# Gated halves added on VectorE and stored plainly, evictions of a down product given out over the next one, the last quarters' running sum on VectorE

## The chip, the cores and the metric

The kernel runs on one core of one Trainium2 chip. The metric is the device time of one execution in microseconds (us); smaller is better. The kernel before takes 1638.05 us (median of three runs, 1633.67 to 1639.48). The execution that the profiler recorded took 1630.3 us, of which 1628.5 us are the span from the first instruction to the last.

A core has five engines with a queue of instructions each: TensorE (PE in the profile; PEld are its weight loads), VectorE (DVE), ScalarE (ACT), GpSimd (POOL) and SyncE (SP). An engine works through its own queue in order; between queues only semaphores order the work. A DMA is issued by one of the queues and runs beside them.

## The reference

One layer of a diffusion backbone: two attention branches over 1024 tokens of 1024 channels, merged and normalized, and then a gated convolutional feed-forward part. Only the feed-forward part and the last normalization are touched:

```python
def _conv_ffn(h, w_up, conv_w, conv_b, w_down):
    u = h @ w_up                                   # 1024 x 1024 @ 1024 x 5632
    u = lax.conv_general_dilated(u, conv_w, ...) + conv_b   # 3 taps along the tokens
    gate, val = jnp.split(u, 2, axis=-1)           # 2816 channels each
    return (jax.nn.silu(gate) * val) @ w_down      # 1024 x 2816 @ 2816 x 1024
...
h = x * (1.0 + scale2) + shift2
y = _conv_ffn(h, w_up[l], conv_w[l], conv_b[l], w_down[l])
x = _layer_norm(DEEPNORM_ALPHA * x + gate2 * y, ln2_g[l], ln2_b[l])
```

All of it is float32. The kernel makes a float32 product of three reduced ones: each operand is split into a high part (a cast on ScalarE) and a low part (a subtraction), and TensorE runs high x high, low x high and high x low (L90, L91, L92 in `mm3`).

## The kernel before

**Up projection.** The 2816 channels of gate and of value are 22 pairs of tiles of 128 channels, j = 0 to 21; a pair is called a tile below. Tiles 0 to 2 are computed directly (`up_conv`). From tile 3 on `up_tile` computes gate, value and both halves of the tokens with seven products of quarter size in place of eight (Strassen's scheme in Winograd's form): A11, S2, S1, S3, A12, S4, A22, each four times three matmuls of 512 columns, 84 for a tile. They land in four banks of PSUM, a, b, c, d. S2 and S1 use operands T2 and T1 that `build` prepares once; T2 and T4 of channel block k stand in the tiles T24h and T24l (high and low), whose cast is L1113. A12 adds to bank a, so it waits until ScalarE has copied A11 out (L1368, `pv<-a`).

Behind its products, a tile needs on VectorE the sums of the banks (L1356), for gate (`tg`) and value (`tv`) the three taps (L1231 on ScalarE, L1232 and L1234 on VectorE), Silu (L1386), and the product of both (L1243 or L1249, in `gated`). On GpSimd it needs one sum (`uv<-uv,pv`, L1356), the low parts of two weights (L87) and four sums of weights for the next tile but one (`s<-ru`, L1075). The raw weights `ru` come by two DMAs of SP (L1325) when their buffers are free.

**Gated values.** For the down projection, which runs in seven products in the same way, DRAM holds the operands: `td[j]` has four slots of 128 x 512 for a tile j below 11. With lo and hi for the two halves of the tokens, slot 0 is lo, slots 1 and 2 are lo+hi, slot 3 is hi. The kernel before writes lo into slots 0, 1 and 2, hi into 3, by SP (L1244, L1245), and then has GpSimd issue a DMA that adds hi to slots 1 and 2 in DRAM (L1247; L1305 for tiles 0 to 2, after all three). That DMA waits until the stores have landed. Tiles 11 to 21 go negated into `g2d`, and GpSimd's DMA (L1251) adds their hi to slots 2 and 3 of tile j-11; it waits only for VectorE's product.

**Down projection.** `product(p)` runs for p = 1, 6, 2, 7, 4, 5, each 11 steps k of four output blocks f, 132 matmuls of 512 columns, into four banks; the next product takes the other four. The seventh product, 3, comes last in two quarters of 256 tokens (`last_mm`, tiles `yl`). For each step two tiles are loaded (`rd`, L1208 and L1209), cast on ScalarE (`hd`, L82) and subtracted on VectorE (`ld`, L87), three steps ahead (`dnext`). The eleven pairs of product 3 are loaded at places that `D3AT` lists as (product, step), the others after product 5. After a product its four banks are evicted: f by f added to the outputs `zz` (L1417 and L1423), with running sums of the values (`zs`, L995, on GpSimd) and of the squares (`zq`, L994 and L996) for the normalization.

**Normalization.** `ln_steps` yields steps (statistics by TensorE, L1028 and L1029; a broadcast, L1044; then for each f L1051 on VectorE, L1053 on GpSimd or VectorE, L1410 on ScalarE and a store) that `tick` interleaves with the matmuls: each has a delay in model nanoseconds (`LN2_D`, 640 of them for three matmuls). The first half of the tokens (b0) runs under product 5. The last 256 tokens are transposed by TensorE (`tok`, tiles `zt`) into banks of product 5.

Only TensorE's queue stands as written. The other queues are ordered by a scheduler that takes instructions as it expects them to be ready. Slots of SBUF (`ht` takes one, `hput` gives it back) go round: who takes a slot waits for its last readers, DMAs among them.

Of the kernel before, what the change touches and what calls it, by code (L numbers as in the profile page):

```python
# [10 lines left out]
ALU = mybir.AluOpType  # L11
# [16 lines left out]
HALF = 512  # L28
# [7 lines left out]
SPAN = 0.8, 0.85  # L36
LN1_F = 3500.0, 2000.0, 2000.0
LN1_D = (2500.0, 2000.0, 2000.0, 2500.0), (2500.0, 2000.0, 1000.0, 700.0), (2500.0, 2000.0, 1000.0, 700.0)
LN2_D = 16000.0, 5000.0, 2500.0, 1500.0, 700.0
LN2_E = 3500.0, 3000.0, 1500.0, 800.0, 500.0  # L40
NCL = 3
BLD = 2400.0
# [3 lines left out]
GORD = 3, 4, 4, 1, 4  # L46
PWB = 5
DAH = 3
D3AT = (7, 1), (7, 4), (7, 7), (4, 1), (4, 4), (4, 7), (5, 0)
NXS = 5  # L50
RAWB = 3
OTP = (0, 0), (1, 0)
# [7 lines left out]
LN2_P = 1, 2, 2  # L60
# [9 lines left out]
def layer_kernel(  # L70
# [6 lines left out]
    nc = tc.nc  # L77
# [44 lines left out]
    NH = NF // 2  # L122
    td = [dpool.tile([P, 4, HALF], F32, tag=f"td{j}", name=f"td{j}") for j in range(NH)]
# [104 lines left out]
    acc = [acc_tile(f"q1acc{t}") for t in range(NT)]  # L228
# [715 lines left out]
    for f in range(2, KT):  # L944
# [4 lines left out]
        for j in range(4):  # L949
            k = (f % 2) * 4 + j  # L950
# [35 lines left out]
    def ln_add(zf, zs, zq, s, first, nm, qe, se):  # L986
        w = s.stop - s.start
        ln_flush()
        if first:
            nc.scalar.activation(zq[:, s], zf, AF.Square)  # L990
            nc.gpsimd.tensor_scalar(out=zs[:, s], in0=zf, scalar1=1.0, scalar2=0.0, op0=ALU.mult, op1=ALU.add)
            return
        q = tm(f"sq{nm}", w=w)
        nc.scalar.activation(q, zf, AF.Square)  # L994
        se.tensor_tensor(out=zs[:, s], in0=zs[:, s], in1=zf, op=ALU.add)  # L995
        sqs.append(lambda: qe.tensor_tensor(out=zq[:, s], in0=zq[:, s], in1=q, op=ALU.add))  # L996
# [204 lines left out]
    def dload(p, k, mk):  # L1201
        w, g = dsrc(p, k)
        n = nraw[0] % (3 + len(xs))
        nraw[0] += 1
        pool, tag, bufs = (post, "raw", 3) if n < 3 else (*xs[n - 3], 1)
        r = pool.tile([P, 2, HALF], F32, tag=tag, name=f"rd{p}_{k}", bufs=bufs)
        o = r[:, 0]
        nc.sync.dma_start(o.rearrange("p (a b) -> p a b", b=P) if len(w.shape) == 3 else o, w)  # L1208
        nc.sync.dma_start(r[:, 1], g)  # L1209
        if p == 2:  # L1210
            nc.gpsimd.dma_start(td[k][:, 2], r[:, 1], accum_op=ALU.add)
        h, l = (mk(f"{a}d{p}_{k}", (P, 2, HALF), R32) for a in "hl")
        split(r, h, l, nc.scalar, nc.vector)
        return h, l
# [22 lines left out]
    def twice(a, n=2):  # L1237
        return a.unsqueeze(1).to_broadcast([P, n, HALF])

    def gated(j, tg, tv):  # L1240
        lo, hi = tg[:, 0:HALF], tg[:, HALF:T]
        if j < NH:
            nc.vector.tensor_tensor(out=tg, in0=tg, in1=tv, op=ALU.mult)  # L1243
            nc.sync.dma_start(td[j][:, 0:3], twice(lo, 3))  # L1244
            nc.sync.dma_start(td[j][:, 3], hi)  # L1245
            if j >= NCL:
                nc.gpsimd.dma_start(td[j][:, 1:3], twice(hi), accum_op=ALU.add)  # L1247
# [53 lines left out]
    for j in range(NCL):  # L1301
        up_conv(j)
    drain()
    for j in range(NCL):
        nc.gpsimd.dma_start(td[j][:, 1:3], twice(td[j][:, 3]), accum_op=ALU.add)  # L1305
    hput(*[f"B{k}_1" for k in range(4)])


# [130 lines left out]

    sides = [banks[0:4], banks[4:8]]  # L1440
    nside = [0]
    d3 = []
    h0, h1 = hsl(0), hsl(1)

    def product(p):
        tags = sides[nside[0] % 2]
        nside[0] += 1
        acc = [ps4.tile([P, HALF], F32, tag=f"r{n}", name=f"p{p}_{f}") for f, n in enumerate(tags)]
        for k in range(NH):
            dnext()  # L1450
# [22 lines left out]
    zs2, zq2 = tm("zs2"), tm("zq2")  # L1473

    def sums(f, s, first):
        ln_add(zv(f, s), zs2, zq2, s, first, f"b{f}_{s.start}", nc.vector, nc.gpsimd)

    for p in (1, 6, 2, 7, 4, 5):
        if p == 6:
            for hf in (0, 1):  # L1480
                for k in range(4):
                    for a in (0, 1):
                        nc.sync.dma_start(zt_[k, hf][:, a], zd[k + 4 * a][:, hsl(hf)])
            for a in (0, 1):
                nc.sync.dma_start(lnr[a], ln2_row[a].partition_broadcast(P))
        if p == 5:
            banks[:] = sides[nside[0] % 2 ^ 1]
        acc = product(p)
        for f in range(4):
            o = acc[f]  # L1490
            if p == 1:
                nc.scalar.copy(u2[f], o)
            elif p == 6:
                accum(f, h0, u2[f], False)
                nc.vector.tensor_tensor(out=u2[f], in0=u2[f], in1=o, op=ALU.subtract)
            elif p == 2:
                accum(f, h0, o, True)
                sums(f, h0, f == 0)
                accum_affine(f, h1, u2[f], True)
            elif p == 7:  # L1500
                nc.vector.tensor_tensor(out=u3[f], in0=u2[f], in1=o, op=ALU.add)
# [8 lines left out]
        if p == 7:  # L1510
            hput("u20", "u21", "u30", "u31")
        if p == 4:
            pend += ln_steps(zs2, zq2, h0, "b0", emit2, *LN2_D, LN2_P[0])
    for f in range(4):
        accum(f, h1, acc[f], True)
    banks[:] = sides[nside[0] % 2] + sides[nside[0] % 2 ^ 1]
    d3 += [dload(3, k, ring) for k in range(len(D3AT), NH)]

    s = LN2_S[-1]
    w = s.stop - s.start  # L1520
# [187 lines left out]
```

## Time and profile before

| | |
|---|---|
| median of three runs | 1638.05 us |
| profiled execution | 1630.3 us, span 1628.5 us |
| PE busy in the span | 1542.9 us (95%) |
| DVE, ACT, POOL busy | 1209.8, 811.2, 721.8 us |
| up projection, tiles 3 to 21 | about 998 to 1395 us from the span's start |
| down products 1, 6, 2, 7, 4, 5 | about 1395 to 1574 us |
| last quarters and output | about 1574 to 1628 us |

In a row of the timeline the first number is the start in us from the span's start, the second the duration; a bracket at the end gives the idle time of the engine ahead of the row and what ended it. Several instructions of one kind in a row are merged (x2). In a row of windows the stretch comes first, then its length, then busy time and number of instructions of PE, PEld, DVE, ACT and POOL, then the granted clock of TensorE, the busy share of the DMA engines and GB/s. Names are those of the program, without numbers.

### The profile page before, as it was taken

To read this page: it belongs to the slowest core of one execution; us is meant where nothing else is said; L and a number is where in the kernel's file an instruction comes from. 1 tells how busy PE (TensorE), PEld (TensorE's weight loads), DVE (VectorE), ACT (ScalarE), POOL (GpSimd) and SP (SyncE) were. 2 spreads that over 40 slices of the span, in tenths; PEclk is the share of its full clock that TensorE was granted. 3 is DMA by queue.
4 is the path that set the end of the run, shared out by engine and by line. 5 is a ranking of instruction groups with operands and counts; after the bars stand their busy time and mean duration, and the time that the engine had idled before them with its cause. 6 is when DMAs were issued, how large, how long until landed. Compare 5 with 4: busy or idle time off the path is not lost.

```text
span 1628.5 us, 22043 instructions
## 1 busy us (share of the span) xinstructions
PE 1542.9 (95%) x7680; PEld 1275.9 (78%) x7680; DVE 1209.8 (74%) x1748; ACT 811.2 (50%) x1443; POOL 721.8 (44%) x749
## 2 busy tenths in 40 slices
PE   6999999999999999999999989999999999999895
PEld 5878788888877887777788877877778888888785
DVE  7796646548887677888756695799988887657775
ACT  5422222368887667787223563434345444445532
POOL 0563303426665556665225344544447664021133
PEclk9999999999999999999999999999999999999998
DMA  9685662322255655531540324344444447997522
GB/s 379 217 315 182 218 202 82 113 78 59 60 147 126 149 123 137 111 68 44 176 155 27 104 78 128 108 108 123 130 104 107 120 114 189 361 266 232 183 96 72
DMA packets 115184, 235.76 MB, mean 145 GB/s; under 512 B 12960, under 2 KB 27808, under 8 KB 114976
## 3 DMA queue, kind: packets, MB, share of 16 engines
q1 hardware_dynamic: 96640, 198.93, 36.6%
q0 software_dynamic: 13392, 25.96, 10.4%
q10 hardware_dynamic: 5040, 9.46, 1.6%
q8 instruction: 60, 0.98, 0.2%
q14 instruction: 52, 0.43, 0.1%
HBM read 178.93 MB, written 71.63 MB: 154 GB/s over the span
## 4 chain that ended last, share of the span: by engine, by line
PE 62%; DVE 17%; DMA 7%; ACT 6%; issue 5%; POOL 3%; SPq 1%; ACTq 0%; DVEq 0%; POOLq 0%
PE ptr L531 4%; DVE tg L1232 4%; PE p L91 3%; PE p L92 2%; PE p L90 2%; PE g L90 2%; PE g L91 2%; PE g L92 2%; PE b L92 2%; PE b L91 2%; PE b L90 2%; DMA wml<-in_wmodT_dram 2%; PE s L414 2%; PE av L552 2%; PE av L553 2%
## 5 line engine op out<-in xcount | busy, mean ns | idle before, releaser
L541 DVE TENSOR_TENSOR ptl<-ptr,pth 128x512 fp32r<-128x512 f32 x188 | 124.6, 684 | 27.8 <-ACT pth L540 25.1
L87 DVE TENSOR_TENSOR ld<-rd,hd 128x1024 fp32r<-128x1024 f32 x77 | 95.0, 1249 | 57.9 <-ACT hd L82 51.5
L531 PE MATMUL ptr<-ident,p 128*128 128x128 f32 x816 | 126.8, 278 | 9.6 <-DVE ptl L541 7.1
L540 ACT CAST pth<-ptr 128x512 fp32r<-128x512 f32 x188 | 106.6, 588 | 56.4 <-PE ptr L531 32.7
L426 ACT ACTIVATE p<-p,nm 128x1024 f32<-128x1024 f32 (+2 forms) x128 | 125.3, 981 | 11.4 <-DVE p L459 10.6
L82 ACT CAST hd<-rd 128x1024 fp32r<-128x1024 f32 x77 | 80.3, 1051 | 98.9 <-PE p L92 73.8
L531 PEld LDWEIGHTS ptr<-ident,p 128*128 128x128 f32 x816 | 93.7, 140 | 40.0 <-DVE ptl L541 14.3
L91 PE MATMUL p<-ld,hd 128*128 128x512 f32 x264 | 103.5, 392 | 5.4 <-DVE ld L87 5.4
L1232 DVE SCALAR_TENSOR_TENSOR tg<-ug,cvt,tg 128x1023 f32<-128x1023 f32 x19 | 88.6, 4665 | 25.4 <-ACT tg L1231 25.4
L552 PE MATMUL av<-pth,VT 128*128 128x512 f32 x236 | 104.6, 443 | 1.0 <-ACT avs L558 0.5
L90 PE MATMUL p<-hd 128*128 128x512 f32 x264 | 103.7, 393 | 0.0
L92 PE MATMUL p<-hd,ld 128*128 128x512 f32 x264 | 103.2, 391 | 0.0
L90 PE MATMUL g<-hh,whg 128*128 128x512 f32 x256 | 99.9, 390 | 0.0
L92 PE MATMUL g<-hh,wlg 128*128 128x512 f32 x256 | 99.7, 389 | 0.0
L91 PE MATMUL g<-hl,whg 128*128 128x512 f32 x256 | 99.6, 389 | 0.0
L553 PE MATMUL av<-ptl,VT 128*128 128x512 f32 x236 | 97.7, 414 | 2.0 <-POOL ptl L87 1.8
L87 POOL TENSOR_TENSOR wlg<-wg,whg 128x512 fp32r<-128x512 f32 x32 | 44.7, 1403 | 110.3 <-ACT whg L82 110.3
L459 DVE TENSOR_SCALAR_CACHE_REDUCE p<-s,cvt,nmc 128x1024 f32<-128x1024 f32 x64 | 84.4, 1339 | 12.3 <-PE s L415 11.8
L414 PE MATMUL s<-KL,q 128*128 128x512 f32 (+2 forms) x192 | 76.0, 396 | 2.9 <-ACT p_x L426 2.0
L188 DVE CUSTOM_DVE_ANT_0 wml<-wml,sc,bmc 128x1024 f32<-128x1024 f32 x32 | 45.2, 1422 | 38.4 <-DMA wml<-in_wmodT_dram 38.2
L90 PE MATMUL a<-B,wA 128*128 128x512 f32 x152 | 61.8, 406 | 11.5 <-ACT pv L1368 11.5
L415 PE MATMUL s<-KL,q 128*128 128x512 f32 (+2 forms) x192 | 71.6, 373 | 0.0
(395 smaller groups left out, 4926.1 us busy)
## 6 DMA issues: line engine op xcount, KB each, us to landing
wml<-in_wmodT_dram SPq DMA_DIRECT2D x48, 512.0 KB
ru<-in_w_up_dram SPq DMA_DIRECT2D x38, 512.0 KB
rd<-td SPq DMA_DIRECT2D x55, 256.0 KB
rd<-sd SPq DMA_DIRECT2D x44, 256.0 KB
td<-tg POOLq DMA_DIRECT2D x19, 512.0 KB, 6.5
rd<-in_w_dn_dram SPq DMA_DIRECT2D x33, 256.0 KB
wm<-in_wmodT_dram SPq DMA_DIRECT2D x16, 512.0 KB
wg<-in_w_g_dram SPq DMA_DIRECT2D x32, 256.0 KB
```

The costliest lines, as they stand in the source:

```text
L87: lo_eng.tensor_tensor(out=lo, in0=src, in1=hi.bitcast(F32), op=ALU.subtract)
L90: nc.tensor.matmul(ps, a[0], b[0], start=start, stop=False, skip_group_check=resumed)
L91: nc.tensor.matmul(ps, a[0], b[1], start=False, stop=False, skip_group_check=resumed)
L92: nc.tensor.matmul(ps, a[1], b[0], start=False, stop=stop, skip_group_check=resumed)
L414: nc.tensor.matmul(o, self.q[0][:, hs], ks, start=True, stop=False)
L426: nc.scalar.activation(p, s, AF.Exp, bias=nm[:, h:h + 1], scale=scale, accum_out=sm[:, h:h + 1])
L531: nc.tensor.transpose(tr[:, h * P:(h + 1) * P], self.pslice(h, n), ident)
L540: nc.scalar.copy(hi, tr)
L541: nc.vector.tensor_tensor(out=lo, in0=tr, in1=hi.bitcast(F32), op=ALU.subtract)
L552: nc.tensor.matmul(self.av, v, hi, start=first, stop=False)
L553: nc.tensor.matmul(self.av, v, lo, start=False, stop=self.left == 0)
L1232: nc.vector.scalar_tensor_tensor(out=t[:, 1:T], in0=u[:, 0:T - 1], scalar=cvw[:, c, 0:1], in1=t[:, 1:T], op0=ALU.mult, op1=ALU.add)
```

## The change

There are three parts and two changed lists.

- `gated` (tiles 0 to 10): VectorE adds lo and hi into the first half of `tv`; SP stores lo into slot 0, hi into slot 3 and the sum into slots 1 and 2. The DMAs that GpSimd issued to add in DRAM (L1247 and L1305) are gone, eleven in all.
- Down products: the four evictions of a product are kept as a list and written into the next product, one at each odd step k (at each step of product 5), behind that step's loads. The normalization of b0 starts when product 4's evictions are given out. The evictions of product 5 are still written out behind it.
- The running sum `zs` of the last two quarters goes from GpSimd to VectorE.
- `LN2_D` and `D3AT` have new values that belong to the second part.

```diff
-LN2_D = 16000.0, 5000.0, 2500.0, 1500.0, 700.0
+LN2_D = 5000.0, 4000.0, 2500.0, 1500.0, 700.0
-D3AT = (7, 1), (7, 4), (7, 7), (4, 1), (4, 4), (4, 7), (5, 0)
+D3AT = (7, 5), (7, 9), (4, 1), (4, 4), (4, 7), (4, 10), (5, 2)
...
         if j < NH:
             nc.vector.tensor_tensor(out=tg, in0=tg, in1=tv, op=ALU.mult)
-            nc.sync.dma_start(td[j][:, 0:3], twice(lo, 3))
+            nc.vector.tensor_tensor(out=tv[:, 0:HALF], in0=lo, in1=hi, op=ALU.add)
+            nc.sync.dma_start(td[j][:, 0], lo)
             nc.sync.dma_start(td[j][:, 3], hi)
-            if j >= NCL:
-                nc.gpsimd.dma_start(td[j][:, 1:3], twice(hi), accum_op=ALU.add)
+            nc.sync.dma_start(td[j][:, 1:3], twice(tv[:, 0:HALF]))
...
-    for j in range(NCL):
-        nc.gpsimd.dma_start(td[j][:, 1:3], twice(td[j][:, 3]), accum_op=ALU.add)
...
             if (p, k) in D3AT:
                 d3.append(dload(3, len(d3), ht))
+            if evict and (k % 2 or p == 5):
+                evict.pop(0)()
+            if not evict and after:
+                after.pop()()
...
-        ln_add(zv(f, s), zs2, zq2, s, first, f"b{f}_{s.start}", nc.vector, nc.gpsimd)
+        ln_add(zv(f, s), zs2, zq2, s, first, f"b{f}_{s.start}", nc.vector,
+               nc.vector if s.start else nc.gpsimd)
...
-        for f in range(4):
-            o = acc[f]
+
+        def ev(f, o, p=p):
             if p == 1:
                 nc.scalar.copy(u2[f], o)
...
+        evict += [lambda f=f, o=acc[f]: ev(f, o) for f in range(4)]
         if p == 4:
-            pend += ln_steps(zs2, zq2, h0, "b0", emit2, *LN2_D, LN2_P[0])
+            after.append(lambda: pend.extend(ln_steps(zs2, zq2, h0, "b0", emit2, *LN2_D, LN2_P[0])))
+    banks[:] = sides[nside[0] % 2] + sides[nside[0] % 2 ^ 1]
+    d3 += [dload(3, k, ring) for k in range(len(D3AT), NH)]
+    for e in evict:
+        e()
     for f in range(4):
         accum(f, h1, acc[f], True)
```

Three places in the queues matter below. The first is ScalarE's queue at the start of tile 3, with what each row waits for in the brackets (`DVE`, `PE`, `Pool`, `Activation` are engines, `DMAHW` are DMAs of SP). `c0_2` and `c1_2` are gate and value of tile 2, `pv3` the copy of tile 3's bank a, T24h_3 the cast of T2 and T4 for channel block 3. Before:

```order
L1231 ACTIVATE c1_2_10449<-u1_2_10386,cvt_70 128x1024 [waits PE_49]
L82 CAST wA11_4_10589<-ru0_4_10565 128x512 [waits DMAHW0_49]
L1113 CAST T24h_3_10467<-t24_3_10460 128x1024 [waits DVE_49,Activation_49]
L1368 COPY pv3_10512<-a3_10508 128x512 [waits PE_49]
L82 CAST wS2_4_10622<-s12_4_10569 128x512 [waits Pool_49]
```

With the change:

```order
L1231 ACTIVATE c1_2_10453<-u1_2_10390,cvt_70 128x1024 [waits PE_49]
L82 CAST wA11_4_10592<-ru0_4_10568 128x512 [waits DMAHW0_49]
L1366 COPY pv3_10515<-a3_10511 128x512 [waits PE_49]
L82 CAST wS2_4_10625<-s12_4_10572 128x512 [waits Pool_49]
L1113 CAST T24h_3_10473<-t24_3_10466 128x1024 [waits DMAHW3_49,DVE_49,Activation_49]
```

The cast of T24h_3 moved behind two rows and gained a wait for a DMA: its slot is that of value tile `c1_2`, which the new store reads.

The second is VectorE's queue where product 7 ends and product 4 begins: `u30`, `u31`, `zz` are evictions of product 7, `ld4_k` the low part for step k of product 4, `ld3_k` for product 3. Before, from the fifth eviction of product 7 on (the four ahead of it follow `ld4_1` and `ld3_5`):

```order
L1417 SCALAR_TENSOR_TENSOR zz1_0_13217<-u30_13225,nmod_13211,zz1_0_13217 128x512
L1423 SCALAR_TENSOR_TENSOR zz1_1_13218<-zz1_1_13218,lnx_69,ya5_14186 128x512
L1501 TENSOR_TENSOR u31_13226<-u21_13224,p7_2_13947 128x512
L1501 TENSOR_TENSOR u31_13226<-u21_13224,p7_3_13948 128x512
L1417 SCALAR_TENSOR_TENSOR zz2_0_13219<-u31_13226,nmod_13211,zz2_0_13219 128x512
L1417 SCALAR_TENSOR_TENSOR zz3_0_13221<-u31_13226,nmod_13211,zz3_0_13221 128x512
L1423 SCALAR_TENSOR_TENSOR zz2_1_13220<-zz2_1_13220,lnx_69,ya6_14191 128x512
L1423 SCALAR_TENSOR_TENSOR zz3_1_13222<-zz3_1_13222,lnx_69,ya7_14196 128x512
L87 TENSOR_TENSOR ld4_2_14207<-rd4_2_14203,hd4_2_14206 128x1024
```

With the change:

```order
L87 TENSOR_TENSOR ld4_1_14168<-rd4_1_14164,hd4_1_14167 128x1024
L1504 TENSOR_TENSOR u30_13236<-u20_13234,p7_0_13927 128x512
L87 TENSOR_TENSOR ld4_2_14191<-rd4_2_14187,hd4_2_14190 128x1024
L1415 SCALAR_TENSOR_TENSOR zz0_0_13226<-u30_13236,nmod_13222,zz0_0_13226 128x512
L1421 SCALAR_TENSOR_TENSOR zz0_1_13227<-zz0_1_13227,lnx_69,ya4_14222 128x512
L87 TENSOR_TENSOR ld4_3_14210<-rd4_3_14206,hd4_3_14209 128x1024
L1504 TENSOR_TENSOR u30_13236<-u20_13234,p7_1_13928 128x512
L1504 TENSOR_TENSOR u31_13237<-u21_13235,p7_2_13929 128x512
```

Before, all twelve evictions stood ahead of `ld4_2`; now one does.

The third is VectorE's queue where product 5 ends (`rbb0` is b0's broadcast, `p5_f` a bank of product 5, `modc` and `nmod` the gains for its two evictions). Before, from the fifth of the eight L1051 on, and then with the change, from the eighth on:

```order
L1051 TENSOR_TENSOR zz0_0_13215<-zz0_0_13215,rbb0_14663 128x512
L1417 SCALAR_TENSOR_TENSOR zz0_1_13216<-p5_0_14453,modc_60,zz0_1_13216 128x512
L1417 SCALAR_TENSOR_TENSOR zz1_1_13218<-p5_1_14454,modc_60,zz1_1_13218 128x512
L1417 SCALAR_TENSOR_TENSOR zz2_1_13220<-p5_2_14455,modc_60,zz2_1_13220 128x512
L1417 SCALAR_TENSOR_TENSOR zz3_1_13222<-p5_3_14456,modc_60,zz3_1_13222 128x512
```

```order
L1051 TENSOR_TENSOR zz3_0_13232<-zz3_0_13232,rbb0_14646 128x512
L1415 SCALAR_TENSOR_TENSOR zz0_1_13227<-p5_0_14444,modc_60,zz0_1_13227 128x512
L87 TENSOR_TENSOR ld3_7_14745<-rd3_7_14741,hd3_7_14744 128x1024
L87 TENSOR_TENSOR ld3_8_14752<-rd3_8_14748,hd3_8_14751 128x1024
L87 TENSOR_TENSOR ld3_9_14759<-rd3_9_14755,hd3_9_14758 128x1024
L87 TENSOR_TENSOR ld3_10_14766<-rd3_10_14762,hd3_10_14765 128x1024
L1415 SCALAR_TENSOR_TENSOR zz1_1_13229<-p5_1_14445,modc_60,zz1_1_13229 128x512
```

All eight L1051 now stand ahead of product 5's first eviction (five before), and the last four `ld3` behind that first one. In ScalarE's queue the casts `hd3_7` to `hd3_10` moved behind the eight output rows of b0 in the same way.

More of the change, by code (lines that the diff above doesn't have):

```diff
@@ L1441, in layer_kernel @@
     nside = [0]
-    d3 = []
+    d3, evict, after = [], [], []
     h0, h1 = hsl(0), hsl(1)
@@ L1503, in layer_kernel @@
                 accum_affine(f + 4, h1, u3[f], False)
+                if f == 3:
+                    hput("u20", "u21", "u30", "u31")
             elif p == 4:
@@ L1509, in layer_kernel @@
                 sums(f + 4, LN2_S[1], f == 0)
-        if p == 7:
-            hput("u20", "u21", "u30", "u31")
+        evict += [lambda f=f, o=acc[f]: ev(f, o) for f in range(4)]
         if p == 4:
-            pend += ln_steps(zs2, zq2, h0, "b0", emit2, *LN2_D, LN2_P[0])
+            after.append(lambda: pend.extend(ln_steps(zs2, zq2, h0, "b0", emit2, *LN2_D, LN2_P[0])))
[3 more added lines that the diff above has]
+        e()
     for f in range(4):
         accum(f, h1, acc[f], True)
-    banks[:] = sides[nside[0] % 2] + sides[nside[0] % 2 ^ 1]
-    d3 += [dload(3, k, ring) for k in range(len(D3AT), NH)]
     s = LN2_S[-1]
```

## Prediction

> **What bounds the kernel now.** First the page's parts on busy time and on the chain that ended last:
>
> ```profile
> PE 1542.9 (95%) x7680; PEld 1275.9 (78%) x7680; DVE 1209.8 (74%) x1748; ACT 811.2 (50%) x1443; POOL 721.8 (44%) x749
> PE 62%; DVE 17%; DMA 7%; ACT 6%; issue 5%; POOL 3%; SPq 1%; ACTq 0%; DVEq 0%; POOLq 0%
> PE ptr L531 4%; DVE tg L1232 4%; PE p L91 3%; PE p L92 2%; PE p L90 2%; PE g L90 2%; PE g L91 2%; PE g L92 2%; PE b L92 2%; PE b L91 2%; PE b L90 2%; DMA wml<-in_wmodT_dram 2%; PE s L414 2%; PE av L552 2%; PE av L553 2%
> ```
>
> TensorE is busy 95% of the span, so all there is to win is in its 85.6 us of gaps and in matmuls that run at a lower clock. One VectorE line, L1232, holds 4% of the chain. So the next view is the windows from one `tg` L1232 to the next, which is one tile of the up projection each (tiles 3, 5, 6, 10, 11; the last row holds the eight tiles 13 to 20):
>
> ```profile
> 1021.41:1040.45 19.04, 19.04 (x85) 15.77 (x84) 14.19 (x14) 9.26 (x13) 10.65 (x8) 1.00 0.47 125
> 1059.49:1080.64 21.15, 19.65 (x86) 15.72 (x85) 19.75 (x14) 8.89 (x13) 9.18 (x8) 1.00 0.44 114
> 1080.64:1103.81 23.17, 20.78 (x85) 16.71 (x84) 20.61 (x14) 8.89 (x13) 11.34 (x11) 0.93 0.47 131
> 1168.04:1191.49 23.45, 20.86 (x85) 16.72 (x84) 20.81 (x15) 8.88 (x13) 11.59 (x11) 0.93 0.50 130
> 1191.49:1212.02 20.53, 19.64 (x86) 15.69 (x85) 19.14 (x14) 8.88 (x13) 11.44 (x10) 1.00 0.44 91
> 1230.96:1383.50 152.54, 152.54 (x674) 126.36 (x673) 126.92 (x110) 72.88 (x101) 98.10 (x60) 1.00 0.50 130
> ```
>
> Tiles 13 to 20 take 152.54/8 = 19.07 us each with TensorE never idle (152.54/674 = 0.226 us a matmul). Tiles 5 to 11 take 20.5 to 23.5 with the same matmuls. Why, the timeline shows at tile 6:
>
> ```profile
> 1077.40 0.68 DVE L1356 TENSOR_TENSOR uv<-d,uv 128x512 f32<-128x512 f32 x1
> 1078.75 0.33 SPq L1325 DMA_DIRECT2D ru<-in_w_up_dram  x1
> 1079.91 1.19 POOL L1247 DMA_DIRECT2D td<-tg  x1 [11.97 <-DMA td<-tg]
> 1080.69 1.74 POOL L1356 TENSOR_TENSOR uv<-uv,pv 128x512 f32<-128x512 f32 x1
> 1088.17 1.68 POOL L1075 TENSOR_TENSOR s<-ru,s 128x512 f32<-128x512 f32 x1
> 1080.64 10.30 DVE L1232 SCALAR_TENSOR_TENSOR tg<-ug,cvt,tg 128x1023 f32<-128x1023 f32 x1 [1.36 <-ACT tg L1231]
> 1090.87 0.68 DVE L1356 TENSOR_TENSOR uv<-d,pv 128x512 f32<-128x512 f32 x1
> 1094.41 0.68 PE L90 MATMUL a<-B,wA 128*128 128x512 f32 x1 [2.39 <-ACT pv L1368]
> 1094.89 0.63 PE L91 MATMUL a<-B,wA 128*128 128x512 f32 x1
> ```
>
> GpSimd stands 11.97 us at its DMA until the stores have landed. Then its seven other rows run without a gap, one each 1.25 us ((1088.17-1080.69)/6), and L1232, which starts 0.05 us before the first of them, lasts 10.30 us: it ends 1.1 us after GpSimd's last. Everything behind it on VectorE is late, so ScalarE's second tap and `pv` behind that, and TensorE waits 2.39 us for `pv`; then its matmuls start every 0.43-0.48 us for a while in place of 0.226. Tile 17 has the same rows without that backlog:
>
> ```profile
> 1303.83 1.59 POOL L1356 TENSOR_TENSOR uv<-uv,pv 128x512 f32<-128x512 f32 x1 [1.05 <-DVE uv L1356]
> 1305.39 1.29 POOL L87 TENSOR_TENSOR wS<-s,wS 128x512 fp32r<-128x512 f32 x1
> 1307.13 1.28 DVE L1232 SCALAR_TENSOR_TENSOR tg<-ug,cvt,tg 128x1023 f32<-128x1023 f32 x1 [1.36 <-ACT tg L1231]
> 1309.43 1.92 POOL L1075 TENSOR_TENSOR s<-ru 128x512 f32<-128x512 f32 x1 [2.75 <-DMA ru<-in_w_up_dram]
> 1304.33 13.54 SPq L1325 DMA_DIRECT2D ru<-in_w_up_dram  x2
> ```
>
> GpSimd's sum follows VectorE's at once, the low part follows, and then GpSimd waits for `ru`, issued at 1304.33 and landed 5.1 us later. In that hole L1232 takes 1.28 us.
>
> **The change, part by part. Gated values, tiles 3 to 12.** The DMA leaves GpSimd's queue. In tile 6 its sum could then start at 1078.1, when VectorE's is done (1077.40 + 0.68), and the low part would end at 1080.6; the hole of tile 17 follows, and L1232 (1080.64) falls into it. VectorE gets one sum of 128x512 more per tile, 0.68 us by the L1356 row. It works 14.2 us of 19.04 in tile 3's window, so TensorE covers it; without cover it would cost 9 x 0.68 = 6.1 us. SP gets a third store, a little under 0.5 us of issue; the next `ru` waits for a split that comes later anyway. From tile 3's L1232 to tile 12's it is 1212.02-1021.41 = 190.6 us now; nine periods of 19.07 are 171.6. Gain **19.0**. If every second tile still stalled, half, 9.5.
>
> The Trainium skill, page "SBUF — State Buffer", section "SBUF: two separate sides", says that VectorE instructions with two SBUF inputs and GpSimd share one port pair by an exclusive lock, held "for the whole instruction". By that rule L1232 would wait for one GpSimd row at most, 1.7 us, and 6.5 of its 10.30 us would have another cause; then this term would be about nil in place of 19.0, which is a rival below. The trace speaks against it: the wait spans all seven rows.
>
> **The price of the stored sum, tile 3.** ScalarE's cast of T24h_3 now waits until the store that reads `c1_2` has landed. Rows at that place (`td<-c` are tile 2's stores):
>
> ```profile
> 1002.69 1.22 DVE L1243 TENSOR_TENSOR c<-c,c 128x1024 f32<-128x1024 f32 x1
> 1004.37 0.48 SPq L1245 DMA_DIRECT2D td<-c  x1
> 1008.81 1.14 POOL L1305 DMA_DIRECT2D td<-td  x1 [9.01 <-DMA td<-c]
> 1004.00 1.04 ACT L1113 CAST T24h<-t 128x1024 fp32r<-128x1024 f32 x1 [3.95 <-DVE c L1243]
> 1005.10 0.50 PE L90 MATMUL b<-T24h,wS 128*128 128x512 f32 x1 [2.33 <-ACT T24h L1113]
> ```
>
> TensorE waits here already. The third store issues behind the second (1004.85) and takes 0.48: 1005.3. Stores landed 1008.81-1004.85 = 4.0 us after their last issue: 1009.3. The cast then starts 5.3 us later than 1004.00, and nothing covers it: **+5.3**. In later tiles the landing took less (tile 6: 1079.91 is 3.3 us after the last issue), `ru` took 5.1: +4.6 to +6.4. Behind the cast on ScalarE stand casts for tile 4, which are not needed for 20 us. T24h_2 and T24l_1 get such waits too, but earlier, and TensorE reaches them 10 us and more later: nil.
>
> **Evictions given out.** The waits of the down stage (1395 to 1628 us), and the windows around product 7's end and the last quarters:
>
> ```profile
> PE p L91 <- DVE ld L87: 5.4, 2, 4.5
> PE stb L1028 <- POOL zs L995: 2.2, 1, 2.2
> 1505.96 1.28 DVE L1501 TENSOR_TENSOR u<-u,p 128x512 f32<-128x512 f32 x2
> 1513.66 5.75 DVE L87 TENSOR_TENSOR ld<-rd,hd 128x1024 fp32r<-128x1024 f32 x5
> 1510.00:1530.00 20.00, 15.49 (x62) 12.37 (x61) 14.31 (x15) 7.92 (x10) 0.00 (x0) 0.91 0.61 203
> 1580.00:1600.00 20.00, 17.40 (x142) 16.91 (x142) 13.54 (x26) 6.18 (x10) 9.28 (x10) 0.99 0.14 52
> ```
>
> Product 7's twelve evictions hold VectorE from 1505.96 to 1513.66, the low parts of product 4 come late, and TensorE waits 4.5 us; with the slow matmuls behind, 62 are done in 20 us where 20/0.226 = 88 fit: 26 x 0.226 = 5.9 us lost. With one eviction (three rows, 2 us) per two steps (5.4 us) between the low parts, which are made two steps ahead, this goes: **-5.9**; if loads of product 3, one more of which falls into product 4, make VectorE wait there, half of it stays, -3. The other wait, 5.4-4.5, follows product 2 and goes too: **-0.9**.
>
> **The end.** VectorE's queue there is worse. Rows now:
>
> ```profile
> 1567.84 0.86 PE bcrb L1044 x2
> 1570.26 7.95 POOL L1053 TENSOR_TENSOR zz<-zz,mbb 128x512 f32<-128x512 f32 x5 [8.00 <-ACT mbb L1046]
> 1571.88 0.82 ACT L1410 ACTIVATE of<-zz,ln2c 128x512 f32<-128x512 f32 x1 [1.70 <-POOL zz L1053]
> 1575.73 2.72 DVE L1417 SCALAR_TENSOR_TENSOR zz<-p,modc,zz 128x512 f32<-128x512 f32 x4
> 1583.41 2.34 DVE L87 TENSOR_TENSOR ld<-rd,hd 128x1024 fp32r<-128x1024 f32 x2
> ```
>
> I count from E, the end of product 5. Now seven passes of three matmuls (4.8 us) and the broadcast (1.7) lie between 1567.84 and E = 1574.3; with the change fourteen passes do, so b0's broadcast starts at E-11.2, GpSimd's L1053 2.4 later (1570.26-1567.84) at E-8.8, and eight of them at 7.95/5 = 1.59 end at E+3.9. ScalarE's last output row ends at E+4.7, then `hd3_7` (1.05) and on VectorE four `ld3` at 1.17 (2.34/2): E+10.4. TensorE needs them after 84 matmuls at 17.40/142 = 0.1225, E+10.3 to E+11.4: just in time. But three more evictions of product 5, with six small sums of about 0.4 between, and two of the other sign, 0.68 each, stand behind them: E+16.2. TensorE wants those two banks for its transposes at E+11.8: a wait of 4.4 us that is not there now. The wait of 2.2 for `zs` goes in exchange, since TensorE comes later than VectorE's sums (eight of 0.4 us, covered by that wait; uncovered 3.2). I take **+2.0**, between -2.4 (old wait gone, none new) and +6 (L1053 slower, and slow matmuls behind).
>
> **Sum.** -19.0 + 5.3 - 5.9 - 0.9 + 2.0 = -18.5. Made against the profiled execution's 1630.3 us it gives 1611.8. The median of the runs shown lies 7.75 above that execution, and the changed kernel will be timed like those, so I forecast 1638.05 - 18.5 = **1619.5 us**.
>
> **Rivals.** *Half the gain*: GpSimd still meets L1232 in every second tile, because `ru` comes at another moment. For it: tiles 7, 9 and 11 stalled less than 6, 8 and 10, so the state of one tile depends on the one ahead. Against it: eight tiles in a row run clean without the store wait. 1638.05 - 9.0 = 1629.
>
> *The lock-out stays and the sum adds to it* (slower side): L1232's length isn't GpSimd's backlog. Place: tiles 4 to 11, VectorE between `ug` and `uv<-d,pv`. It decides if `ru` lands less than 1.9 us (1080.6-1078.75, SP's issue behind the split in tile 6) after its issue, or if one row's hold was never the cause. Then the 19.0 are lost and the extra sum lies on the stalled path, +6.1: 5.3 - 5.9 - 0.9 + 2.0 + 6.1 = +6.6, 1644.7, and 1648.7 with the end at its upper bound. Against it: 5.1 us in the `ru` row. The "SBUF — State Buffer" page's rule would lead here.
>
> *The prices don't come*: the cast at tile 3 and the end are hidden. -25.8, which is 1612, less some of the -2.4: 1611. For it: my count at the end rests on rows of other moments.
>
> *It doesn't do what it says* for evictions (the scheduler puts them ahead of the loads again): the order in VectorE's queue excludes this for product 4.
>
> **Chances.** Forecast 0.72, half the gain 0.10, prices don't come 0.13, lock-out stays 0.05. About 0.5% (8 us) is what a measurement of this kernel can tell from no change. Faster by more: forecast, third rival and most of the first, 0.90; within: the rest of the first and half of the second, 0.07; slower: 0.03. The range is 1608 to 1630: below, all gains, no end price and the fastest run's base (1633.67); above, half the gain.
>
> **What would show it.** Right: `tg` L1232 at 1.3-1.6 us in all tiles from 3, periods of 19.0-19.1, no wait for `pv`; a wait for T24h_3 of 7-8 us; in product 4 no wait for `ld`; a wait of some 4 us at the first transposes. Wrong: L1232 rows of 7 us and more, or waits on DMAs (`rd`) in products 7 and 4.

## The result and the profile after

The changed kernel takes 1611.8 us (median of four runs, 1607.43 to 1612.16), the kernel before 1635.86 us beside it (median of four, 1633.06 to 1639.48). The ratio is 0.985, with a 95% interval of 0.982 to 0.987: the change wins 21 to 30 us. The forecast was 1619.5 us, with a range of 1608 to 1630.

The profiled execution of the changed kernel took 1612.16 us, its span is 1610.4 us, 18.1 less than before's 1628.5. First the page's parts on busy time and on the chain that ended last, after the change:

```profile
PE 1536.3 (95%) x7680; PEld 1275.4 (79%) x7680; DVE 1197.2 (74%) x1766; ACT 814.6 (51%) x1443; POOL 745.3 (46%) x731
PE 73%; DVE 10%; ACT 4%; issue 4%; DMA 4%; POOL 3%; SPq 0%; ACTq 0%; DVEq 0%; POOLq 0%
```

TensorE's share of the chain rose from 62% to 73%, VectorE's fell from 17% to 10%. The row of L1232 in the groups by line (columns: how many, shortest, median and longest in ns, first and last start in us), before and then after:

```profile
L1232 DVE SCALAR_TENSOR_TENSOR tg<-ug,cvt,tg x19: 1283/1332/10508, 1021.4 to 1383.5; 128x1023 f32<-128x1023 f32 x19
```

```profile
L1232 DVE SCALAR_TENSOR_TENSOR tg<-ug,cvt,tg x19: 1283/1284/2365, 1029.4 to 1372.3; 128x1023 f32<-128x1023 f32 x19
```

The longest fell from 10.5 to 2.4 us. The windows from tile 3's L1232 to tile 12's, after the change:

```profile
1029.36:1200.72 171.36, 171.36 (x757) 141.94 (x756) 147.52 (x135) 83.33 (x117) 113.49 (x63) 1.00 0.33 109
```

TensorE works through all of these 171.36 us; before they were 190.6. The waits of TensorE after the change, from 1010 us to the end (us in total, times, longest):

```profile
PE b L90 <- ACT T24h L1113: 6.5, 1, 6.5
PE b L91 <- DVE T24l L1075: 0.5, 1, 0.5
PE zt L1538 <- DVE zz L1415: 4.0, 3, 3.4
```

These three are all that is left: no `pv`, no `ld`, no `zs`. Two prices stand there, the stored sum at tile 3 (6.5, it was 2.33) and the first transposes (4.0).

Where the 18.1 us went, from the first and last starts of TensorE's groups before and after. `u` is the direct up convolution of tiles 0 to 2, `p` the six down products, from 1 to 5 in the order in which they run, `yl` the last quarters. Before:

```profile
L90 PE MATMUL u<-B,hwu x120: 280/389/628, 918.7 to 997.2; 128*128 128x512 f32 x72, 128*128 128x256 f32 x48
L90 PE MATMUL p<-hd x264: 388/389/793, 1383.8 to 1573.5; 128*128 128x512 f32 x132
L90 PE MATMUL yl<-hd x88: 278/283/469, 1574.2 to 1613.3; 128*128 128x256 f32 x88
```

After:

```profile
L90 PE MATMUL u<-B,hwu x120: 278/389/767, 922.1 to 1000.4; 128*128 128x512 f32 x72, 128*128 128x256 f32 x48
L90 PE MATMUL p<-hd x264: 389/389/793, 1372.5 to 1555.0; 128*128 128x512 f32 x132
L90 PE MATMUL yl<-hd x88: 277/283/561, 1555.7 to 1595.4; 128*128 128x256 f32 x88
```

| stretch | before | after | difference | forecast |
|---|---|---|---|---|
| to the last `u` (unchanged code) | 997.2 | 1000.4 | +3.2 | 0 |
| last `u` to L1232 of tile 3 | 24.2 | 29.0 | +4.8 | +5.3 |
| L1232 of tile 3 to that of tile 12 | 190.6 | 171.4 | -19.2 | -19.0 |
| products 1 to 5 (first to last `p`) | 189.7 | 182.5 | -7.2 | -6.8 |
| last `p` to the end of the span | 55.0 | 55.4 | +0.4 | +2.0 |

What is left, from tile 12 to product 1, takes 171.8 us in both. The changed stretches sum to -21.2, and 3.2 come back in code that the change doesn't touch. (The rows give 0.1 us, so a difference can be off by as much. The products begin at 1383.8 us in the kernel before, not at about 1395 as the table of its stages has it.)

### The profile page after: what moved, and what is told of

The parts are those of the page before. It is cut to its first block, busy times and chain, and to the rows that moved or that the text cites. A ratio compares the mean times of both kernels' runs of the same rounds, so it can differ in the third digit from the quotient of the medians.

```text
span 1610.4 us, 22060 instructions
## 1 busy us (share of the span) xinstructions
PE 1536.3 (95%) x7680; PEld 1275.4 (79%) x7680; DVE 1197.2 (74%) x1766; ACT 814.6 (51%) x1443; POOL 745.3 (46%) x731
## 4 chain that ended last, share of the span: by engine, by line
PE 73%; DVE 10%; ACT 4%; issue 4%; DMA 4%; POOL 3%; SPq 0%; ACTq 0%; DVEq 0%; POOLq 0%
PE ptr L531 4%; PE p L92 4%; PE p L91 4%; PE p L90 4%; PE b L92 3%; PE b L91 3%; PE b L90 3%; PE g L90 2%; PE g L91 2%; PE g L92 2%; PE c L90 2%; PE c L92 2%; PE c L91 2%; PE d L90 2%; PE d L92 2%
## 5 line engine op out<-in xcount | busy, mean ns | idle before, releaser
L541 DVE TENSOR_TENSOR ptl<-ptr,pth 128x512 fp32r<-128x512 f32 x188 | 124.8, 686 | 27.7 <-ACT pth L540 25.4
L84 POOL TENSOR_SCALAR pth<-prw 128x512 fp32r<-128x512 f32 x48 | 31.2, 650 | 87.8 <-ACT prw L537 62.2
L82 ACT CAST wA<-ru 128x512 fp32r<-128x512 f32 x57 | 35.6, 625 | 71.4 <-PE d L92 33.7
```

The costliest lines, as they stand in the source:

```text
L82: nc.scalar.copy(hi, src)
L541: nc.vector.tensor_tensor(out=lo, in0=tr, in1=hi.bitcast(F32), op=ALU.subtract)
```

## The experiments

### The parts alone

*Gated values alone* (VectorE's sum and three plain stores in the kernel before):

```diff
+            nc.vector.tensor_tensor(out=tv[:, 0:HALF], in0=lo, in1=hi, op=ALU.add)
-            nc.sync.dma_start(td[j][:, 0:3], twice(lo, 3))
+            nc.sync.dma_start(td[j][:, 0], lo)
...
-                nc.gpsimd.dma_start(td[j][:, 1:3], twice(hi), accum_op=ALU.add)
+            nc.sync.dma_start(td[j][:, 1:3], twice(tv[:, 0:HALF]))
```

> The kernel before with the gated part alone: VectorE's sum and three plain stores, no DMA on GpSimd for tiles 0 to 10; evictions and sums as before. Theory (GpSimd's stand at its DMA backs its rows up, and L1232 is locked out until they are through): L1232 at 1.3 to 1.6 us in all 19 tiles, -19.0 from tile 3 to tile 12; the cast of T24h_3 waits for the store, +5.3 (the changed kernel's trace has +4.7); sum -14, ratio about 0.9914. Rival (the lock-out has another cause and the sum adds to it): L1232 still 7 to 10 us, 5.3 + 6.1 = +11.4, ratio 1.007.

Measured: 1620.32 us against 1635.63, ratio 0.9916 (0.9885 to 0.9946), which is 13.7 us by the ratio. L1232 is at 1.28 us except in tiles 4 and 5 (2.36 and 2.20), tile 3 to tile 12 takes 171.36 us, TensorE waits 6.5 us for T24h_3. Both terms, the gain and its price, are there in their sizes.

*Evictions, sums and lists alone* (the changed kernel with the old `gated`, which is the first diff turned round):

> The changed kernel with the old gated part (GpSimd adds in DRAM): so the given-out evictions, the sums and the two lists alone against the kernel before. Theory: L1232 as before (up to 10.5 us), no wait for ld in product 4, sum -5.9 - 0.9 + 2.0 = -4.8 (the changed kernel's trace has -7.2 in the products and +0.4 behind them, so -6.8), ratio 0.996 to 0.997. Rival (the two parts help each other): within 2 us of before, and the gain of both parts is more than the sum of e1 and e2.

Measured: 1626.17 us, ratio 0.9947 (0.9929 to 0.9966), 8.7 us by the ratio. In its trace the products take as long as in the changed kernel, 182.5 us, and L1232 is locked out as before (up to 10.28 us):

```profile
L90 PE MATMUL p<-hd x264: 389/389/793, 1389.7 to 1572.2; 128*128 128x512 f32 x132
PE zt L1540 <- DVE zz L1417: 4.1, 3, 3.4
```

The gain of the parts adds up: 13.7 + 8.7 = 22.4 us, within the interval of the whole change. The rival of mutual help is not needed.

*The sums alone* (running sum of the last two quarters on VectorE, in the kernel before):

```diff
-        ln_add(..., nc.vector, nc.gpsimd)
+        ln_add(..., nc.vector, nc.vector if s.start else nc.gpsimd)
```

> The kernel before with the third part alone: the running sum of the last two quarters on VectorE. The prediction took the wait of 2.2 us for that sum out and put VectorE's 8 x 0.4 us under it: -2.2 to +1 us, ratio 0.9985 to 1.0006. Rival (VectorE's queue at the end is the bound, so the sums lie on the path): +3 us, ratio 1.002.

Measured: 1635.31 us against 1635.5, ratio 0.9995 (0.9979 to 1.0010): nothing. The wait did not go, it changed its name; before it was `POOL zs L995: 2.2`:

```profile
PE stb L1028 <- DVE zs L995: 2.0, 1, 2.0
```

So GpSimd was not the main cause. In the kernel before, its last sum waits for an eviction of the last quarters and then takes 0.72 us, a third of the 2.2:

```profile
1596.80 0.72 POOL L995 TENSOR_TENSOR zs<-zs,zz 128x256 f32<-128x256 f32 x1 [0.82 <-DVE zz L1417]
```

With the sum on VectorE it stands in the queue that was late already.

### What locks L1232 out

The prediction said: GpSimd stands at its DMA, its rows pile up, run without a gap, and a run without a gap locks L1232 out. Five kernels take that apart.

*The DMA one tile later*, so that its stores have long landed (kernel before):

```diff
-            if j >= NCL:
-                nc.gpsimd.dma_start(td[j][:, 1:3], twice(hi), accum_op=ALU.add)
+            if j > NCL:
+                nc.gpsimd.dma_start(td[j - 1][:, 1:3], twice(td[j - 1][:, 3]), accum_op=ALU.add)
```

> The kernel before, but GpSimd issues the DMA that adds hi to slots 1 and 2 of a tile 3 to 10 one tile later, when the stores have long landed. The DMAs and their traffic stay, the stand goes. Theory (it is the stand that backs GpSimd up): L1232 at 1.3 us, or 2 to 4 us where the 1.2 us of the DMA's issue and one low part lie in its way; -12 to -19 from tile 3 to 12, nothing at T24h_3, ratio 0.988 to 0.993. Rival (the adding DMA itself, its issue or its traffic, locks L1232 out): L1232 stays at 7 to 10 us, ratio 1.000.

Measured: 1621.11 us, ratio 0.9918 (0.9893 to 0.9943), -13.4 us: inside the expected gain. But not as expected. GpSimd still waits about 1 us at the DMA, and the lock-out doesn't go, it moves. VectorE and GpSimd at tile 6:

```profile
1077.19 1.61 POOL L1358 TENSOR_TENSOR uv<-uv,pv 128x512 f32<-128x512 f32 x1 [10.28 <-DVE uv L1358]
1079.89 1.14 POOL L1247 DMA_DIRECT2D td<-td  x1 [1.09 <-DMA td<-tg]
1080.65 1.72 POOL L87 TENSOR_TENSOR wS<-s,wS 128x512 fp32r<-128x512 f32 x1
1087.01 1.57 POOL L1075 TENSOR_TENSOR s<-ru,s 128x512 f32<-128x512 f32 x1
1079.61 1.28 DVE L1232 SCALAR_TENSOR_TENSOR tg<-ug,cvt,tg 128x1023 f32<-128x1023 f32 x1 [1.36 <-ACT tg L1231]
1080.81 0.69 DVE L1358 TENSOR_TENSOR uv<-d,pv 128x512 f32<-128x512 f32 x1
1081.41 8.25 DVE L1234 SCALAR_TENSOR_TENSOR tg<-ug,cvt,tg 128x1023 f32<-128x1023 f32 x1
```

L1232 falls into GpSimd's wait ahead of the DMA and takes 1.28 us. Behind the DMA GpSimd's six rows run one each 1.27 us ((1087.01 - 1080.65)/5), and now the next tap, L1234, lasts 8.25 us: it ends 1.1 us after GpSimd's last. In tiles 4 and 5, where L1232 comes behind the DMA, it still takes 6.96 and 9.50 us, where 2 to 4 were expected. The gain comes from L1234 standing less in TensorE's way than L1232 did: TensorE's waits for `pv` between 1000 and 1220 us are 11.5 us before and 3.4 here. The windows from tile 6 to tile 12:

```profile
1079.61:1198.77 119.16, 117.26 (x506) 93.68 (x505) 110.76 (x84) 53.69 (x78) 63.74 (x50) 1.00 0.50 129
```

That is 119.16/6 = 19.9 us a tile, where the kernel before has 20.5 to 23.5.

*A stand without a DMA* (changed kernel, GpSimd waits for the stores by a copy of one column):

```diff
             nc.sync.dma_start(td[j][:, 1:3], twice(tv[:, 0:HALF]))
+            if j >= NCL:
+                nc.gpsimd.tensor_copy(tv[:, 0:1], lo[:, 0:1])
```

> The changed kernel with one more GpSimd instruction per tile 3 to 10: a copy of one column that must wait until the new stores have landed, so GpSimd stands there without issuing a DMA. Theory (the stand and the gapless rows behind it): L1232 at 6 to 10 us again in tiles 4 to 11, +10 to +19 against the changed kernel, ratio to before 0.991 to 0.997. Rival (the adding DMA itself): L1232 at 1.3 us, ratio as the changed kernel's 0.985. Rival (a lock is held for one GpSimd instruction): L1232 at most 1.3 + 1.7 = 3.0 us, not more than +5.

Measured: 1610.47 us, ratio 0.9855 (0.9830 to 0.9880), as the changed kernel; L1232 at most 2.40 us. This doesn't test the theory: the copy landed behind GpSimd's sum in the queue, where the stores had nearly always landed, and GpSimd waited there 2.2 us in all eight tiles together. It shows only that the column copy costs nothing. What a stand of GpSimd without a DMA would do stays untested.

*Rows that pile up without a DMA*, and *the same with a DMA in between*. Both are the changed kernel with four more sums on GpSimd, whose result nothing uses. In the second GpSimd also issues the third store:

```diff
+            for _ in range(4 * (j >= NCL)):
+                nc.gpsimd.tensor_tensor(out=tv[:, HALF:T], in0=lo, in1=hi, op=ALU.add)
```

```diff
-            nc.sync.dma_start(td[j][:, 1:3], twice(tv[:, 0:HALF]))
+            (nc.gpsimd if j >= NCL else nc.sync).dma_start(td[j][:, 1:3], twice(tv[:, 0:HALF]))
```

> The changed kernel with four more GpSimd sums of 128x512 in each tile 3 to 10, right behind the product of gate and value; their result is not used. They end about when L1232 of the next tile becomes ready, so GpSimd's own seven rows run behind them without a gap, as in the kernel before, but without a DMA on GpSimd's queue. Theory as predicted (any unbroken run of GpSimd rows locks L1232 out): L1232 at 7 to 10 us in tiles 4 to 11, +15 to +20 against the changed kernel, ratio to before 0.995 to 0.998. New rival (rows run over each other, and lock VectorE out, only behind a DMA that GpSimd has issued; without one VectorE takes turns with it row by row, as tile 4 of the changed kernel shows with L1232 at 2.37 us): GpSimd's rows end before the next begins, L1232 at most 3.7 us, other VectorE rows of two SBUF inputs at 1.7 to 2.4 us, +0 to +5, ratio 0.984 to 0.988.

> As the run with four more GpSimd sums per tile 3 to 10, and the store of the sum into slots 1 and 2 is issued by GpSimd in place of SP: a plain store that adds nothing in DRAM and waits for VectorE's sum alone. It stands behind the third of the four extra sums, so one of them and GpSimd's seven own rows follow it at once. Predicted theory: as the run without the DMA, L1232 at 7 to 10 us in both. New rival (the DMA's issue starts the unbroken run): behind the DMA GpSimd's rows last 1.7 us at 1.25 us spacing, and L1232, or where it comes ahead of the DMA the two-input row behind it, is locked out for 6 to 10 us; ratio 0.993 to 0.999, at least 8 us more than without the DMA.

Measured without the DMA: 1632.63 us, ratio 0.9984 (0.9968 to 1.0001). L1232 takes 1.50 to 1.53 us in tiles 4 to 11, so nothing is locked out. GpSimd and VectorE at tile 6:

```profile
1086.60 6.34 POOL L1249 TENSOR_TENSOR tv<-tg 128x512 f32<-128x512 f32 x4 [1.83 <-DVE tg L1243]
1092.90 1.73 POOL L1356 TENSOR_TENSOR uv<-uv,pv 128x512 f32<-128x512 f32 x1
1094.59 1.27 POOL L87 TENSOR_TENSOR wS<-s,wS 128x512 fp32r<-128x512 f32 x1
1088.37 3.45 DVE L87 TENSOR_TENSOR wS<-s,wS 128x512 fp32r<-128x512 f32 x2
1095.45 1.50 DVE L1232 SCALAR_TENSOR_TENSOR tg<-ug,cvt,tg 128x1023 f32<-128x1023 f32 x1 [1.36 <-ACT tg L1231]
PE d L90 <- DVE uv L1356: 12.8, 6, 2.8
```

GpSimd runs six rows there without a gap. Yet VectorE gets in between them: two low parts of 0.68 us take 3.45 together, so each waits about 1 us, one GpSimd row, and GpSimd's rows in their turn grow from 1.25 to 1.6 us. The engines take turns, row by row. TensorE waits 12.8 us in six tiles for a sum of VectorE that these rows delay (the last line, from the waits between 1040 and 1200 us), and with the slow matmuls behind it tile 3 to tile 12 takes 192.1 us, where the changed kernel takes 171.4; the new rival had expected 5 at most. The prediction's cause, an unbroken run of rows, is not enough for a lock-out, though the time came out about where that cause had put it (ratio 0.995 to 0.998).

With the DMA: 1654.14 us, ratio 1.0117 (1.0080 to 1.0153), 21.5 us more. The same place at tile 6:

```profile
1091.16 4.66 POOL L1249 TENSOR_TENSOR tv<-tg 128x512 f32<-128x512 f32 x3 [1.83 <-DVE tg L1243]
1095.77 0.72 POOL L1247 DMA_DIRECT2D td<-tv  x1
1096.52 1.29 POOL L1249 TENSOR_TENSOR tv<-tg 128x512 f32<-128x512 f32 x1
1097.75 1.28 POOL L1356 TENSOR_TENSOR uv<-uv,pv 128x512 f32<-128x512 f32 x1
1098.99 1.27 POOL L87 TENSOR_TENSOR wS<-s,wS 128x512 fp32r<-128x512 f32 x1
1104.41 1.29 POOL L1075 TENSOR_TENSOR s<-ru 128x512 f32<-128x512 f32 x1 [4.15 <-DMA ru<-in_w_up_dram]
1105.66 2.27 POOL L1075 TENSOR_TENSOR s<-ru,ru 128x512 f32<-128x512 f32 x1
1092.93 3.45 DVE L87 TENSOR_TENSOR wS<-s,wS 128x512 fp32r<-128x512 f32 x2
1096.90 3.92 DVE L87 TENSOR_TENSOR wA<-ru,wA 128x512 fp32r<-128x512 f32 x1
```

Ahead of the DMA the two engines take turns (4.66 us for three rows, 3.45 for two). Behind it GpSimd's three rows take 1.28 each and VectorE's low part, begun at 1096.90, lasts 3.92 us, to 0.6 us after GpSimd is done (1098.99 + 1.27). Then GpSimd waits for `ru`, and behind that gap the turns are back (2.27). The same low part takes 3.92 to 4.08 us in all eight tiles; without the DMA, at the same place, it took 1.15 at tile 6. What changes between the two ways is the DMA that GpSimd issued. The DMA didn't wait for anything and adds nothing in DRAM. Expected were 6 to 10 us of lock-out; it was 3.2 us more than the row needs, since `ru` came late and only three rows followed. The rows don't run over each other here either (1.28 us at 1.24 spacing), so the 1.7 us of the rows in the kernel before is no mark of it.

*A DMA on GpSimd with a gap behind it* (the changed kernel with the second of these two diffs and no extra sums):

> The changed kernel, with the store of the sum into slots 1 and 2 issued by GpSimd in tiles 3 to 10: a plain store that waits for VectorE's sum alone, in GpSimd's queue ahead of its own sum. That sum waits for VectorE about 1 us later, so GpSimd has a gap right behind the DMA. If the DMA's issue starts the unbroken run and a gap ends it: L1232 at 1.3 to 2.4 us, ratio as the changed kernel's, 0.984 to 0.988. If any DMA on GpSimd's queue costs its issue or a lock-out by itself: L1232 of more than 4 us or +8 us and more against the changed kernel, ratio from 0.990.

Measured: 1609.98 us, ratio 0.9841 (0.9815 to 0.9867), as the changed kernel. L1232 is at 1.28 us in every tile from 3. GpSimd at tile 6:

```profile
1076.84 0.72 POOL L1247 DMA_DIRECT2D td<-tv  x1 [3.41 <-issue]
1078.21 1.66 POOL L1354 TENSOR_TENSOR uv<-uv,pv 128x512 f32<-128x512 f32 x1 [0.65 <-DVE uv L1354]
1082.47 1.60 POOL L1075 TENSOR_TENSOR s<-ru 128x512 f32<-128x512 f32 x1 [1.34 <-DMA ru<-in_w_up_dram]
1084.04 2.27 POOL L1075 TENSOR_TENSOR s<-ru,ru 128x512 f32<-128x512 f32 x1
```

So a DMA on GpSimd's queue costs nothing by itself. Behind it come 0.65 us of idle time, two rows that meet no waiting two-input row of VectorE, and a second gap of 1.34; behind that, the 2.27 shows that the engines take turns. Whether the first gap alone would be enough, this run doesn't tell.

In the up projection of these traces, then, a lock-out begins with a DMA that GpSimd issues and ends at GpSimd's next gap; everything that is ready in between runs ahead of VectorE's two-input rows. The kernel before had both: the DMA, and by the stand at it seven rows with no gap. Why the DMA has this effect, the runs don't show. Nor is it so everywhere. In the attention part of the kernel before, GpSimd issues a DMA and eight rows follow, each within 0.1 us of the one ahead; among them are:

```profile
617.67 1.21 POOL L601 DMA_DIRECT2D sd<-in_w_dn_dram  x1 [0.37 <-DMA sd<-sd]
620.35 1.29 POOL L87 TENSOR_TENSOR ptl<-prw,pth 128x512 fp32r<-128x512 f32 x1
622.28 0.79 POOL L87 TENSOR_TENSOR qs<-Q,qs 128x256 fp32r<-128x256 f32 x1
620.40 2.06 DVE L563 TENSOR_TENSOR ot<-avs,up 64x256 f32<-64x256 f32 x2
```

VectorE's L563 also reads two tiles of SBUF, and usually takes 0.42 us. Here the first of the two takes 1.53, about one GpSimd row more, and both are done while four of the eight rows are still to end. GpSimd's rows there are shorter and of other kinds; which of this matters is open.

### The two prices, and a faster version

*Tiles 0 to 2 as before* (changed kernel; for them two stores by SP and the adding DMA by GpSimd, so that no store reads `c1_2`):

```diff
+            if j < NCL:
+                nc.sync.dma_start(td[j][:, 0:3], twice(lo, 3))
+                nc.sync.dma_start(td[j][:, 3], hi)
+                return
...
+    for j in range(NCL):
+        nc.gpsimd.dma_start(td[j][:, 1:3], twice(td[j][:, 3]), accum_op=ALU.add)
```

*The end in another order* (changed kernel; all evictions of product 5 ahead of the last four loads, its sums behind them):

```diff
-                sums(f + 4, LN2_S[1], f == 0)
...
-    d3 += [dload(3, k, ring) for k in range(len(D3AT), NH)]
     for e in evict:
         e()
     for f in range(4):
         accum(f, h1, acc[f], True)
+    d3 += [dload(3, k, ring) for k in range(len(D3AT), NH)]
+    for f in range(4):
+        sums(f + 4, LN2_S[1], f == 0)
```

Both, and the changed kernel again, ran on one chip:

> The changed kernel once more, on the chip of the next three, so that they are compared with it on one chip: ratio to before 0.984 to 0.988.

> The changed kernel with the gated part as before in tiles 0 to 2 alone (two stores by SP, the adding DMA by GpSimd behind tile 2): the value tile of tile 2 is read by no store, so the cast of T24h_3 waits for VectorE's product alone. Theory: the wait of TensorE for T24h_3 falls from 6.5 to about 2.3 us, first L1232 4.7 us earlier, -4 to -5.5 against the changed kernel. Rival (GpSimd's DMA there backs it up and locks VectorE out in tile 4): L1232 of tile 4 at 7 us, and the gain falls to 0 to -3.

> The changed kernel with the end written in another order: all eight evictions of product 5 ahead of the last four low parts of product 3, its sums behind them. Theory (TensorE waits 3.4 us at the transposes for an eviction that stands behind four low parts and sums): that wait goes and no wait for ld comes, -3 to -4.5 us against the changed kernel. Rival (the low parts come late now, or the sums of squares): a wait for ld or for the statistics takes its place, -1 to +2.

> Both of the last two edits on the changed kernel. Theory: the sum of both, -7 to -10 against the changed kernel, ratio to before 0.978 to 0.982, faster than both kernels. Rival (one of them only moves a wait): -3 to -5.

| kernel | median us | ratio to before | from last `u` to L1232 of tile 3 | `yl`, first to last |
|---|---|---|---|---|
| changed, again | 1614.98 | 0.9872 (0.9849 to 0.9894) | 29.7 | 40.1 |
| tiles 0 to 2 as before | 1605.71 | 0.9821 (0.9796 to 0.9846) | 25.4 | 40.0 |
| end in another order | 1607.29 | 0.9826 (0.9803 to 0.9850) | 29.6 | 34.9 |
| both | 1601.75 | 0.9799 (0.9777 to 0.9820) | 22.9 | 34.9 |

Both together are 13.2 us faster than the changed kernel and the fastest measured, 2.0% under the kernel before. What they were to take away is gone in the traces. The waits for T24h_3 with tiles 0 to 2 as before, and the waits of TensorE from 1380 us on with the new order, are:

```profile
PE b L90 <- ACT T24h L1113: 2.3, 1, 2.3
```

```profile
PE zt L1539 <- DVE zz L1415: 0.4, 1, 0.4
PE yl L91 <- DVE ld L87: 0.3, 1, 0.3
```

The last quarters take 34.9 us with the new order, where the changed kernel's two profiles have 39.7 (1555.7 to 1595.4) and 40.1: about 5 us, a wait of 3.4 and the slow matmuls behind it. By median the two edits gave 9.3 and 7.7 us, more than the 4.2 and 5 that these places show; together 13.2. Each single edit's surplus is of the size by which the unchanged start differs from one execution to the next (last `u` at 1002.4 in the changed kernel's second profile, at 996.6 with tiles 0 to 2 as before).

GpSimd's DMA behind tile 2 didn't lock VectorE out in tile 4, as the rival had it (L1232 there 2.42 us with that edit alone, 1.70 with both): it is issued at 1008.26 and GpSimd idles 5.9 us behind it.

## Why the prediction was right, and where it was not

- **Tiles 3 to 12**, -19.0: -19.2 in the trace. The size holds, and so does the place. The reason holds by half. That any run without a gap locks L1232 out was the step that fell: without a DMA a run without a gap makes VectorE take turns (the kernel with four more sums). The lock-out took the DMA and the pile of rows behind it, and the change removed both. That the size held all the same is luck in part. Which one alone would have given the gain isn't shown: a DMA with gaps behind it cost nothing (1609.98 us), and more rows with no DMA cost about as much as the lock-out had (1632.63 us), by turns. The prediction read the two apart in no row, since in the up projection of before every backlog stood behind a DMA.
- **The rule of the Trainium skill** ("SBUF — State Buffer", section "SBUF: two separate sides": the pair of ports is held for one whole instruction) was set aside by the prediction because one wait spanned seven rows. (By that rule 7.3 of the 10.30 us, 10.30 - 1.28 - 1.7, would have another cause, not 6.5 as the prediction has it; nothing else rests on that figure.) Without a DMA ahead it is what the traces show: L1232 at 2.37 us in tile 4 of the changed kernel, 1.1 us of it a wait for one GpSimd row. Behind a DMA in the up projection it doesn't hold: 8.25 us across six rows, 3.92 across three. The rival built on it, that the 19 us would stay, was wrong nevertheless.
- **The stored sum at tile 3**, +5.3 (4.6 to 6.4): +4.8 in the pair of traces. Over all profiles, the eight in which the cast waits for the store take 29.0 to 29.75 us from the last `u` to L1232 (mean 29.4), the six in which it doesn't take 22.9 to 25.8 (mean 24.5): +5.0. The wait of TensorE is 6.5, below the 7 to 8 that were announced: the store landed 2.9 us after its last issue, not 4.0:

```profile
1008.08 0.39 SPq L1247 DMA_DIRECT2D td<-c  x1
1011.40 1.05 ACT L1113 CAST T24h<-t 128x1024 fp32r<-128x1024 f32 x1 [6.29 <-DMA td<-c]
1012.50 0.80 PE L90 MATMUL b<-T24h,wS 128*128 128x512 f32 x1 [6.50 <-ACT T24h L1113]
```

- **Evictions**, -5.9 - 0.9 = -6.8: -7.2, and no wait for `ld` is left in product 4 or elsewhere.
- **The end**, +2.0 (-2.4 to +6): +0.4. The wait at the transposes is there, 3.4 us where 4.4 were counted. The old wait went in exchange, but GpSimd was not its main cause: with the sum on VectorE alone it stayed at 2.0. VectorE's queue was worked out rightly, and its remedy is the order that the faster version has.
- **The base.** The sum of -18.5 against the profiled 1630.3 us gives 1611.8, the median that came. That it fits to 0.1 us is luck: the changed stretches give -21.2, and 3.2 came back in unchanged code. The forecast added the 7.75 us by which before's median lay above its profiled execution, and that step failed: the profiled execution of the changed kernel, 1612.16, lies at its median. On the chip where the changed kernel was run again, the kernel before spreads over 15 us (1628.66 to 1643.41, nine runs), the changed one over 5 (1610.6 to 1615.24, five runs). Whether the locked-out tiles make that spread, as they take 20.5 to 23.5 us in one execution, or the start does, is open. The one other profile near it is that of the sums alone, a kernel as fast as before by the runs: it is 10.9 us longer (1639.4 against 1628.5), of which 4.9 stand ahead of the last `u` and 1.4 in tiles 3 to 12. In that pair the start weighs more.

The rivals: *half the gain* and *the lock-out stays* fell with L1232 at 1.28 us in 18 tiles of 19. *The prices don't come* gave 1611, a hair from the median, for a wrong reason: both prices are in the trace.

## What to carry to other kernels

Look for a DMA on GpSimd's queue with rows ready behind it, next to a VectorE instruction that is several times its usual length: move the DMA to another queue, or put it where GpSimd idles behind it. Before a stored buffer goes round, see who takes it next: a plain store can cost more at one place (here 5 us, once) than it saves in each tile, and one exception for that place gets it back. A wait is named after the instruction that came last: when the sum moved from one engine to another, the wait of 2 us stayed, because most of it came from the evictions a step further up.

## What was not expected of the hardware

In the up projection, a GpSimd that issues a DMA and has rows ready behind it locks out VectorE's instructions with two SBUF inputs until its next gap: 3.9 us over three rows, 8.25 over six, 10.3 over seven. The DMA need not wait, nor add. Without it the engines take turns, a row of 1.25 us growing to 2.27 and one of 1.28 to 2.4, and even that cost TensorE 20 us in the eight tiles with four more sums. The attention part has a place where VectorE gets in behind a DMA after one row, so the DMA isn't the whole condition. The "SBUF — State Buffer" page of the Trainium skill, section "SBUF: two separate sides", tells of the opposite case, a DMA from GpSimd's queue that starves while VectorE holds the ports in one of its two-port modes; no run here shows that one.
